# Mixture of eight expert MLPs on one core: x in four loads of 1, 1, 2 and 4 experts, stores in pairs, late results stored on the GpSimd queue

## The chip, the cores and the metric

The kernel runs on one core of a Trainium2 chip. The metric is device time in microseconds (us), the median of several executions. Five executions of the kernel before took 183.25 to 184.44 us, with a median of 184.28.

## What is computed

Eight experts each apply a two-layer MLP to their own 256 rows. Everything is float32 in memory.

```python
n_experts, capacity, hidden, expert_hidden = 8, 256, 512, 2048
# x: (8, 256, 512)   w1: (8, 512, 2048)   w2: (8, 2048, 512)
h = np.matmul(x, w1)
h = np.maximum(h, 0)
out = np.matmul(h, w2)          # (8, 256, 512) float32
```

## The kernel before

**Data and types.** The matmuls run in bf16. A weight matrix is 4.2 MB of float32 in memory; a DMA issued from GpSimd (`nc.gpsimd.dma_start`, POOL in the profile) converts it to bf16 on the way, so that 2048 KB arrive on the chip. `load_w1` (L60) and `load_w2` (L66) each issue such a load, into pools of three buffers (`WB = 3`). `load_w2` cuts the matrix of expert 6 into 3 pieces and that of expert 7 into 7, the last three of one k-tile (128 KB on the chip) each; all others are one load.

**x.** The eight experts' x is treated as two groups of four experts (`G = 2`). Group 0, 2 MB of float32, is loaded by SP (L132) into `x_f`, 16 KB in a row for each partition, and ACT converts it to bf16 in four casts (L142). Group 1 is loaded and converted by a GpSimd DMA (L137). `transpose_x` (L74) turns a group around on TensorE: 32 transposes of 128x128 for a group, and two copies (L87 on ACT, L89 on DVE) for each of four k-tiles, into `xt`.

**Compute.** `first_layer(e)` (L91) makes 64 matmuls of 128x256 (L97) for an expert; DVE and ACT take turns at the ReLU (L105, L107). `second_layer(e)` (L111) makes 32 matmuls of 128x512 (L117) over 16 k-tiles; DVE and ACT each copy one half of the result (L125, L126) into `o_sb[e]`, from a pool of five buffers.

**Order.** The schedule is written out by hand (`manual_schedule`): each engine executes its instructions in program order, and each queue takes its DMAs in the order of issue. All weights, x group 1 and the results of experts 0 to 4 (`store`, L128) share the one GpSimd queue, called q0 in the profile; SP's queue is q1 and ACT's q10. The order on GpSimd is: w1(0), the identity matrix (two short instructions), w2(0), w1(1), x group 1, w2(1), w1(2), w2(2); then w1(3), w2(3), store 0, w1(4), w2(4), store 1, w1(5), w1(6), w1(7), w2(5), store 2, w2(6) in pieces, store 3, store 4, w2(7) in pieces. A load into a used buffer waits until the matmuls that read it are done, and a DMA on GpSimd also waits for the landing of the eighth DMA before it on this queue, or of a later one, since eight semaphores are used in turn.

TensorE runs the layers expert by expert up to first layer 4, second layer 4, then first layers 5, 6, 7, then second layers 5, 6, 7. The four transposed k-tiles of x group 1 stand between the matmuls of first layer 2.

**The end.** The results of experts 5 and 6 are stored by SP (L179), with a dependency by hand on the third last weight piece, `pieces[-3]`; the result of expert 7 goes out in halves, from SP (L188) and ACT (L189).

Of the kernel before, what the change touches and what calls it, by code (L numbers as in the profile page):

```python
# [1 line left out]

# [5 lines left out]


@with_exitstack  # L10
def kernel(
    ctx: ExitStack,
    tc: tile.TileContext,
    x: bass.AP,
    w1: bass.AP,
    w2: bass.AP,
    out: bass.AP,
):
    nc = tc.nc
    P = 128  # L20
    bf = mybir.dt.bfloat16
    f32 = mybir.dt.float32
    relu = mybir.ActivationFunctionType.Relu

    E, C, H = x.shape
    F = w1.shape[2]
    MT = C // P
    KT1 = H // P
    KT2 = F // P
    G = 2  # L30
    EG = E // G
    J = EG * C // P
    J2 = J // MT
    WB = 3


    x_r = x.rearrange("(g e) c k -> g (e c) k", g=G).rearrange(
        "g (p j) k -> g p j k", p=P
    )
    w1_r = w1.rearrange("e (p kt) n -> e p kt n", p=P)  # L40
    w2_r = w2.rearrange("e (p kt) n -> e p kt n", p=P)
    out_r = out.rearrange("e (p mt) n -> e p mt n", p=P)

    const = ctx.enter_context(tc.tile_pool(name="const", bufs=1))
    wpool = ctx.enter_context(tc.tile_pool(name="weights", bufs=WB))
    hpool = ctx.enter_context(tc.tile_pool(name="hidden", bufs=3))
    opool = ctx.enter_context(tc.tile_pool(name="outs", bufs=5))
    ps_h = ctx.enter_context(tc.tile_pool(name="ps_h", bufs=4, space=bass.MemoryType.PSUM))
    ps_o = ctx.enter_context(tc.tile_pool(name="ps_o", bufs=4, space=bass.MemoryType.PSUM))


    ctx.enter_context(tc.manual_schedule())

    w1_sb, w2_sb, ht, o_sb = {}, {}, {}, {}
    x_f = const.tile([P, J, H], f32, name="x_f")
    x_b = [const.tile([P, J, H], bf, name=f"x_b{g}") for g in range(G)]
    xt = [const.tile([P, KT1, EG, C], bf, name=f"xt{g}") for g in range(G)]
    identity = const.tile([P, P], bf, name="identity")

    def load_w1(e):  # L60
        w1_sb[e] = wpool.tile([P, KT1, F], bf, tag="w1", name="w1_sb")
        nc.gpsimd.dma_start(w1_sb[e][:], w1_r[e])  # L62

    pieces = []

    def load_w2(e):  # L66
        w2_sb[e] = wpool.tile([P, KT2, H], bf, tag="w2", name="w2_sb")
        cuts = {E - 2: (0, 6, 11, 16), E - 1: (0, 4, 8, 11, 13, 14, 15, 16)}.get(e, (0, KT2))
        for lo, hi in zip(cuts, cuts[1:]):
            pieces.append(  # L70
                nc.gpsimd.dma_start(w2_sb[e][:, lo:hi, :], w2_r[e, :, lo:hi, :])  # L71
            )

    def transpose_x(g, kts):  # L74


        for kt in kts:
            pt = ps_o.tile([P, J, P], bf, tag="ps_o", name="pt_tr")
            for j in range(J):
                nc.tensor.transpose(pt[:, j, :], x_b[g][:, j, kt::KT1], identity[:])  # L80
            src = pt[:].rearrange("p (j m) (e l) -> p m e l j", m=MT, e=EG)
            for mt in range(MT):
                dst = xt[g][:, kt, :, mt * P:(mt + 1) * P].rearrange(
                    "p e (l j) -> p e l j", j=J2
                )
                if mt % 2:
                    nc.scalar.copy(dst, src[:, mt])  # L87
                else:
                    nc.vector.tensor_copy(dst, src[:, mt])  # L89

    def first_layer(e, between=()):  # L91
        ht[e] = hpool.tile([P, KT2, C], bf, tag="ht", name="ht_sb")
        for g in range(KT2 // 2):
            ph = ps_h.tile([P, 2, C], f32, tag="ps_h", name="pt_h")
            for i in range(2):
                for kt in range(KT1):
                    nc.tensor.matmul(  # L97
                        ph[:, i, :],
                        w1_sb[e][:, kt, 2 * g + i::KT2],
                        xt[e // EG][:, kt, e % EG, :],  # L100
                        start=(kt == 0),
                        stop=(kt == KT1 - 1),
                    )
            if g % 2:
                nc.vector.tensor_relu(ht[e][:, 2 * g:2 * g + 2, :], ph[:])  # L105
            else:
                nc.scalar.activation(ht[e][:, 2 * g:2 * g + 2, :], ph[:], relu)  # L107
            if g % 2 and between:
                between.pop(0)()

    def second_layer(e):  # L111
        po = [
            ps_o.tile([P, H], f32, tag="ps_o", name=f"pt_o{mt}") for mt in range(MT)
        ]
        for kt in range(KT2):
            for mt in range(MT):
                nc.tensor.matmul(  # L117
                    po[mt][:],
                    ht[e][:, kt, mt * P:(mt + 1) * P],
                    w2_sb[e][:, kt, :],  # L120
                    start=(kt == 0),
                    stop=(kt == KT2 - 1),
                )
        o_sb[e] = opool.tile([P, MT, H], f32, tag="o", name="out_sb")
        nc.vector.tensor_copy(o_sb[e][:, 0, :], po[0][:])  # L125
        nc.scalar.copy(o_sb[e][:, 1, :], po[1][:])  # L126

    def store(e):  # L128
        nc.gpsimd.dma_start(out_r[e], o_sb[e][:])  # L129


    nc.sync.dma_start(x_f[:], x_r[0])  # L132
    load_w1(0)
    make_identity(nc, identity)
    load_w2(0)
    load_w1(1)
    nc.gpsimd.dma_start(x_b[1][:], x_r[1])  # L137
    load_w2(1)
    load_w1(2)
    load_w2(2)  # L140
    for j in range(0, J, 2):
        nc.scalar.copy(x_b[0][:, j:j + 2, :], x_f[:, j:j + 2, :])  # L142
    transpose_x(0, range(KT1))

    first_layer(0)
    load_w1(3)
    second_layer(0)
    load_w2(3)
    store(0)
    first_layer(1)  # L150
    load_w1(4)
    second_layer(1)
    load_w2(4)
    store(1)
    first_layer(2, [lambda kt=kt: transpose_x(1, [kt]) for kt in range(KT1)])
    load_w1(5)
    second_layer(2)
    first_layer(3)
    load_w1(6)
    second_layer(3)  # L160
    first_layer(4)
    load_w1(7)
    load_w2(5)
    store(2)
    load_w2(6)
    store(3)
    second_layer(4)
    store(4)
    load_w2(7)


    for e in (5, 6, 7):
        first_layer(e)
    for e in (5, 6, 7):
        second_layer(e)


    for e in (5, 6):
        d = nc.sync.dma_start(out_r[e], o_sb[e][:])  # L179
        tc.add_manual_dep(  # L180
            d.ins,
            pieces[-3].ins.name,
            mybir.DependencyInfo(
                mybir.DependencyClass.Sync, mybir.DependencyReason.SCHED_ONLY
            ),
            reason="after the weights",
        )
    nc.sync.dma_start(out_r[7, :, 0, :], o_sb[7][:, 0, :])  # L188
    nc.scalar.dma_start(out_r[7, :, 1, :], o_sb[7][:, 1, :])  # L189


# [1 line left out]
_INS = ['x', 'w1', 'w2']  # L193
_OUTS = [((8, 256, 512), 'float32')]


# [23 lines left out]
```

## Time and profile before

| | |
|---|---|
| median of five executions | 184.28 us (183.25 to 184.44) |
| the profiled execution | 184.44 us |
| its span, first to last instruction | 182.2 us |
| mean granted TensorE clock | 0.911 of full speed |
| moved by DMA, as counted on the chip's side | 41.00 MB, mean 225 GB/s |
| read from memory; written to it | 71.30 MB; 4.19 MB |
| share of the 16 DMA engines: q0 (GpSimd); q1 (SP); q10 (ACT) | 93.9%; 5.0%; 0.4% |
| x_f, SP's load of x: issue to landing | 12.7 us |
| w1(0), the first weights: issue at 1.24 us, to landing | 17.0 us |
| first matmul of first layer 0 | 20.13 us |
| last weight piece: issue at 165.87 us, to landing | 11.0 us |
| last matmuls of second layer 7 | end at 178.12 us |
| ACT's half of result 7: issue at 178.76 us, to landing | 2.6 us |

Some execution time lies outside the span: 184.44 against 182.2 here. In the profile's rows an instruction's line number is that of the kernel file. The 40 slices of part 2 cover 4.55 us each; PEclk is the clock that TensorE was granted, and the DMA row the mean busy share of the 16 DMA engines, both in tenths. GB/s counts a converted weight with the bytes that arrive, half of those that are read. The DMA share can exceed 1 a little, because an engine's packets overlap. A DMA issue (DMA_DIRECT2D) on POOL takes about 0.53 us of that engine; the transfer itself follows on the queue.

### The profile page before, as it was taken

The numbers are of one execution on the slowest core, as the hardware profiler recorded it, in microseconds if no ns is written. First come the engines' busy times: TensorE is split into PE (matmuls) and PEld (weight loads), VectorE is DVE, ScalarE is ACT, GpSimd is POOL, SyncE is SP. The second block draws the span as 40 slices with busy tenths as digits, with TensorE's granted clock in tenths as the row PEclk, the third lists the DMA queues.
The fourth block names the chain that finished last, engine by engine and source line by source line (L and its number), as shares of the span: only waits on it lengthen the run. The fifth ranks groups of instructions, "written<-read, shape, count | busy, mean of one in ns | idle before, by whom it ended". The sixth has DMA issues, their size and how long they took to land.

```text
span 182.2 us, 1878 instructions
## 1 busy us (share of the span) xinstructions
PE 131.3 (72%) x825; PEld 91.0 (50%) x832; DVE 32.8 (18%) x48; ACT 33.4 (18%) x53; POOL 16.7 (9%) x36
## 2 busy tenths in 40 slices
PE   0004899759039998949968299937999597996890
PEld 0002795359013597418833279416998495442340
DVE  0000541113100155011301014010343033011001
ACT  2008531113000135011301022011223031011001
POOL 7200001110100101000000000601010101112000
PEclk9999999999956999996999759995799799999698
DMA  6999999999999999999899999999999999999986
GB/s 198 309 259 212 230 223 205 207 212 239 205 209 227 223 216 198 227 227 223 190 274 212 201 230 277 212 205 227 223 219 194 227 230 244 213 279 256 205 202 232
DMA packets 5047, 41.00 MB, mean 225 GB/s; under 512 B 560, under 2 KB 944, under 8 KB 2992
## 3 DMA queue, kind: packets, MB, share of 16 engines
q0 software_dynamic: 4320, 37.23, 93.9%
q1 hardware_dynamic: 576, 3.41, 5.0%
q10 hardware_dynamic: 144, 0.26, 0.4%
q8 instruction: 6, 0.10, 0.2%
q14 instruction: 1, 0.01, 0.0%
HBM read 71.30 MB, written 4.19 MB: 414 GB/s over the span
## 4 chain that ended last, share of the span: by engine, by line
DMA 57%; PE 33%; another core or an unknown queue 5%; POOL 1%; issue 1%; ACT 0%; POOLq 0%
DMA w_sb<-in_w_dram 57%; PE pt_o L117 18%; PE pt_h L97 14%; PE pt_tr L80 1%; POOL w_sb L62 1%; ACT out_sb L126 0%; POOL w_sb L71 0%; POOL x_b L137 0%; POOL identity masks.py:199 0%; POOL identity masks.py:197 0%; POOLq masks.py:199 0%; POOLq L71 0%; POOLq L204 0%
## 5 line engine op out<-in xcount | busy, mean ns | idle before, releaser
L97 PE MATMUL pt_h<-xt,w_sb 128*128 128x256 bf16 x512 | 66.5, 295 | 17.0 <-DMA w_sb<-in_w_dram 16.1
L97 PEld LDWEIGHTS <-w_sb 128*128 128x128 bf16 x512 | 60.3, 148 | 23.8 <-DMA w_sb<-in_w_dram 18.8
L117 PE MATMUL pt_o<-w_sb,ht_sb 128*128 128x512 bf16 x249 | 59.9, 397 | 13.6 <-DMA w_sb<-in_w_dram 13.1
L117 PEld LDWEIGHTS <-ht_sb 128*128 128x128 bf16 x256 | 25.9, 102 | 45.8 <-issue 16.8
L105 DVE TENSOR_SCALAR ht_sb<-pt_h 128x512 bf16<-128x512 f32 x32 | 22.1, 692 | 61.3 <-PE pt_h L97 61.3
L107 ACT ACTIVATE ht_sb<-pt_h 128x512 bf16<-128x512 f32 x32 | 19.1, 598 | 54.4 <-PE pt_h L97 54.4
L80 PE MATMUL pt_tr<-identity,x_b 128*128 128x128 bf16 x64 | 6.6, 264 | 16.2 <-ACT x_b L142 16.2
L126 ACT COPY out_sb<-pt_o 128x512 f32<-128x512 f32 x8 | 4.7, 586 | 71.9 <-PE pt_o L117 71.9
L125 DVE COPY out_sb<-pt_o 128x512 f32<-128x512 f32 x8 | 5.5, 692 | 66.2 <-PE pt_o L117 66.2
L80 PEld LDWEIGHTS <-x_b 128*128 128x128 bf16 x64 | 5.4, 127 | 16.9 <-ACT x_b L142 16.9
L71 POOL DMA_DIRECT2D w_sb<-in_w_dram x16 | 8.6, 541 | 50.4 <-DMA w_sb<-in_w_dram 26.1
L62 POOL DMA_DIRECT2D w_sb<-in_w_dram x8 | 4.4, 552 | 81.4 <-PE pt_h L97 80.6
L89 DVE COPY xt<-pt_tr 128x512 bf16<-128x512 bf16 x8 | 5.5, 686 | 18.3 <-PE pt_tr L80 18.3
L142 ACT CAST x_b<-x_f 128x1024 bf16<-128x1024 f32 x4 | 3.9, 1042 | 11.4 <-DMA x_f<-in_x_dram 11.4
L87 ACT COPY xt<-pt_tr 128x512 bf16<-128x512 bf16 x8 | 4.7, 585 | 7.0 <-DVE xt L89 7.0
L129 POOL DMA_DIRECT2D out_dram<-out_sb x5 | 2.7, 539 | 17.6 <-DMA w_sb<-in_w_dram 17.0
L142 ACT ACT_TABLE_LOAD x1 | 1.3, 1283 | 0.7 <-PEq L204 0.7
L137 POOL DMA_DIRECT2D x_b<-in_x_dram x1 | 0.5, 547 | 0.0
masks.py:199 POOL TENSOR_SCALAR_AFFINE_SELECT identity<-identity 128x128 bf16<-128x128 bf16 x1 | 0.3, 287 | 0.1
masks.py:197 POOL MEMSET identity<- 128x128 bf16 x1 | 0.2, 223 | 0.0
L204 POOL MEMSET const-float32-0.0<- 128x1 f32 x1 | 0.1, 98 | 0.2 <-issue 0.2
L204 POOL MEMSET const-bfloat16-1.0<- 128x1 bf16 x1 | 0.1, 101 | 0.0
(2 smaller groups left out, 0.2 us busy)
## 6 DMA issues: line engine op xcount, KB each, us to landing
w_sb<-in_w_dram POOLq DMA_DIRECT2D x14, 2048.0 KB, 49.6
out_dram<-out_sb POOLq DMA_DIRECT2D x5, 512.0 KB, 41.0
x_f<-in_x_dram SPq DMA_DIRECT2D x1, 2048.0 KB, 12.7
w_sb<-in_w_dram POOLq DMA_DIRECT2D x2, 640.0 KB, 46.6
x_b<-in_x_dram POOLq DMA_DIRECT2D x1, 1024.0 KB, 39.8
w_sb<-in_w_dram POOLq DMA_DIRECT2D x2, 512.0 KB, 21.9
out_dram<-out_sb SPq DMA_DIRECT2D x2, 512.0 KB, 3.1
w_sb<-in_w_dram POOLq DMA_DIRECT2D x1, 768.0 KB, 42.8
```

The lines of the kernel that those rows point to most:

```text
L62: nc.gpsimd.dma_start(w1_sb[e][:], w1_r[e])
L71: nc.gpsimd.dma_start(w2_sb[e][:, lo:hi, :], w2_r[e, :, lo:hi, :])
L80: nc.tensor.transpose(pt[:, j, :], x_b[g][:, j, kt::KT1], identity[:])
L87: nc.scalar.copy(dst, src[:, mt])
L89: nc.vector.tensor_copy(dst, src[:, mt])
L97: nc.tensor.matmul(ph[:, i, :], w1_sb[e][:, kt, 2 * g + i::KT2], xt[e // EG][:, kt, e % EG, :], start=(kt == 0), stop=(kt == KT1 - 1),)
L105: nc.vector.tensor_relu(ht[e][:, 2 * g:2 * g + 2, :], ph[:])
L107: nc.scalar.activation(ht[e][:, 2 * g:2 * g + 2, :], ph[:], relu)
L117: nc.tensor.matmul(po[mt][:], ht[e][:, kt, mt * P:(mt + 1) * P], w2_sb[e][:, kt, :], start=(kt == 0), stop=(kt == KT2 - 1),)
L125: nc.vector.tensor_copy(o_sb[e][:, 0, :], po[0][:])
L126: nc.scalar.copy(o_sb[e][:, 1, :], po[1][:])
L142: nc.scalar.copy(x_b[0][:, j:j + 2, :], x_f[:, j:j + 2, :])
```

## The change

Four things change.

- **x** comes in four groups, of 1, 1, 2 and 4 experts. Group 0, 512 KB of float32, is loaded by SP, 4 KB in a row for each partition, and converted by one cast on ACT. Groups 1, 2 and 3 are GpSimd loads that convert, each into a buffer of its own, placed behind w1(0), behind w1(1) and behind w2(1). Each group is transposed by itself: group 1 after first layer 0, group 2 after first layer 1, group 3 between the matmuls of first layer 2. An expert has the same bytes of x and as many transposes as before.
- **Stores** of experts 0 and 1, 2 and 3, 4 and 5 are joined into one DMA each, from an output buffer for two experts (a pool of four such buffers instead of five single ones).
- **Results of 4, 5 and 6** are stored on the GpSimd queue after all pieces of w2(7); expert 4's store stood ahead of w2(7), and 5 and 6 were on SP. The dependency by hand goes. Expert 7 is stored as before.
- **Pieces**: w2(6) comes in 2 pieces instead of 3, w2(7) in 6 (5, 4, 3, 2, 1, 1 k-tiles) instead of 7.

The order of the GpSimd queue becomes w1(0), x1, w2(0), w1(1), x2, w2(1), x3, w1(2), w2(2), w1(3), w2(3), w1(4), w2(4), store 0+1, w1(5), w1(6), w1(7), w2(5), store 2+3, w2(6), w2(7), store 4+5, store 6. With the same eight semaphores, w2(2) is now the ninth DMA and waits for the landing of w1(0). The matmuls, their sizes and their order are those of before, except for the place of the transposes.

```diff
-    G = 2
-    EG = E // G
-    J = EG * C // P
-    J2 = J // MT
+    GROUPS = ((0, 1), (1, 1), (2, 2), (4, 4))
+    STORES = ((0, 1), (2, 3), (4, 5), (6,), (7,))
...
-    out_r = out.rearrange("e (p mt) n -> e p mt n", p=P)
+    out_r = out.rearrange("e (p mt) n -> p e mt n", p=P)
...
-    opool = ctx.enter_context(tc.tile_pool(name="outs", bufs=5))
+    opool = ctx.enter_context(tc.tile_pool(name="outs", bufs=4))
...
-    x_f = const.tile([P, J, H], f32, name="x_f")
+    x_f = const.tile([P, MT, H], f32, name="x_f")
...
+    def x_rows(g):
+        e0, n = GROUPS[g]
+        return x[e0:e0 + n].rearrange("e c k -> (e c) k").rearrange(
+            "(p j) k -> p j k", p=P
+        )
+
+    def load_x(g):
+        nc.gpsimd.dma_start(x_b[g][:], x_rows(g))
...
-        cuts = {E - 2: (0, 6, 11, 16), E - 1: (0, 4, 8, 11, 13, 14, 15, 16)}.get(e, (0, KT2))
+        cuts = {E - 2: (0, 8, 16), E - 1: (0, 5, 9, 12, 14, 15, 16)}.get(e, (0, KT2))
...
-        o_sb[e] = opool.tile([P, MT, H], f32, tag="o", name="out_sb")
-        nc.vector.tensor_copy(o_sb[e][:, 0, :], po[0][:])
-        nc.scalar.copy(o_sb[e][:, 1, :], po[1][:])
+        es = next(es for es in STORES if e in es)
+        if e == es[0]:
+            o_sb[es] = opool.tile([P, 2, MT, H], f32, tag="o", name="out_sb")
+        o = o_sb[es][:, e - es[0]]
+        nc.vector.tensor_copy(o[:, 0, :], po[0][:])
+        nc.scalar.copy(o[:, 1, :], po[1][:])
...
-    nc.sync.dma_start(x_f[:], x_r[0])
+    nc.sync.dma_start(x_f[:], x_rows(0))
     load_w1(0)
     make_identity(nc, identity)
+    load_x(1)
     load_w2(0)
     load_w1(1)
-    nc.gpsimd.dma_start(x_b[1][:], x_r[1])
+    load_x(2)
     load_w2(1)
+    load_x(3)
     load_w1(2)
     load_w2(2)
-    for j in range(0, J, 2):
-        nc.scalar.copy(x_b[0][:, j:j + 2, :], x_f[:, j:j + 2, :])
-    transpose_x(0, range(KT1))
+    nc.scalar.copy(x_b[0][:], x_f[:])
+    transpose_x(0)
...
-    store(2)
+    store(2, 3)
     load_w2(6)
-    store(3)
     second_layer(4)
-    store(4)
     load_w2(7)
...
-    for e in (5, 6, 7):
-        second_layer(e)
-    for e in (5, 6):
-        d = nc.sync.dma_start(out_r[e], o_sb[e][:])
-        tc.add_manual_dep(
...
+    second_layer(5)
+    store(4, 5)
+    second_layer(6)
+    store(6)
+    second_layer(7)
+    o = o_sb[(7,)]
+    nc.sync.dma_start(out_r[:, 7, 0, :], o[:, 0, 0, :])
+    nc.scalar.dma_start(out_r[:, 7, 1, :], o[:, 0, 1, :])
```

## The prediction

> **What bounds the kernel now.** I read the page first: the shares of part 1, the 40 slices of part 2, the chain of part 4.
>
> ```profile
> PE 131.3 (72%) x825; PEld 91.0 (50%) x832; DVE 32.8 (18%) x48; ACT 33.4 (18%) x53; POOL 16.7 (9%) x36
> ...
> PE   0004899759039998949968299937999597996890
> ...
> DMA  6999999999999999999899999999999999999986
> ...
> DMA 57%; PE 33%; another core or an unknown queue 5%; POOL 1%; issue 1%; ACT 0%; POOLq 0%
> ```
>
> TensorE is busy 72% of the span, but the DMA row is 8 or 9 in every slice except the first and the last. The chain names weight loads for 57%. So the 16 DMA engines are the bound from the first load to the last store, and work on other engines is worth nothing unless it changes when those engines have something to do. The change moves the same bytes (x 4.19 MB read, results 4.19 MB written, weights 67.1 MB read as f32), so only idle DMA time and order can change the end. I therefore asked for the DMA share by stretches at both ends (columns: length, the engines' busy time, PEclk, DMA share, GB/s):
>
> ```profile
> 0.00:1.70 1.70, 0.00 (x0) 0.00 (x0) 0.00 (x0) 0.97 (x1) 0.67 (x5) 1.00 0.00 0
> 1.70:3.20 1.50, 0.00 (x0) 0.00 (x0) 0.00 (x0) 0.32 (x1) 1.43 (x5) 1.00 1.07 240
> 3.20:5.40 2.20, 0.00 (x0) 0.00 (x0) 0.00 (x0) 0.00 (x0) 2.20 (x5) 1.00 0.98 410
> ...
> 174.40:176.40 2.00, 2.00 (x11) 0.88 (x9) 0.00 (x0) 0.00 (x0) 0.00 (x0) 1.00 0.45 73
> 176.40:179.20 2.80, 1.71 (x8) 0.59 (x6) 0.69 (x1) 0.59 (x1) 0.00 (x0) 1.00 0.94 375
> 179.20:181.10 1.90, 0.00 (x0) 0.00 (x0) 0.00 (x0) 0.00 (x0) 0.00 (x0) 0.87 0.74 276
> ```
>
> DMA is busy from 1.7 us. The only soft places are 174.4 to 176.4 (0.45) and the last two microseconds (0.74). Then I asked which queue fills the first stretch (DMA view of 1.7 to 5.4, then of 5.5 to 6 us):
>
> ```profile
> q1 hardware_dynamic: 77, 1.26, 101.5%
> ```
>
> ```profile
> q0 software_dynamic: 12, 0.20, 185.7%
> q1 hardware_dynamic: 2, 0.03, 15.8%
> ```
>
> Up to 5.4 us every packet belongs to the SP load of x; the GpSimd queue (q0), which carries all weights, shows its first packets only then, although its first issue stands at 1.24 us:
>
> ```profile
> 0.74 0.37 SPq L132 DMA_DIRECT2D x_f<-in_x_dram  x1
> 1.24 0.66 POOL L62 DMA_DIRECT2D w_sb<-in_w_dram  x1 [0.79 <-POOLq L204]
> ```
>
> The 2 MB load of x is thus what the engines live on before the weights come.
>
> **The change part by part.**
>
> *The first load of x, 512 KB instead of 2 MB.* At the rates above it moves 1.5 us x 240 GB/s = 0.36 MB by 3.2 us and the other 0.16 MB in 0.4 us: done at 3.6 us. If the first weights still come at 5.4, the DMA engines idle 1.8 us, and the 0.74 MB of x that moved in that time in the old kernel must be moved later, on a stream that is full. A packet of 16 KB takes 16384 x 16 / 410 GB/s = 0.64 us, and q0 had to wait on average half of one for its turn, 0.3 us, which a free engine doesn't need. I take **+1.5 us**. Both ends: nothing (q0 was ready by 3.6 and only sat behind x packets already under way) and +2.4 us (q0 gets its first turn when the opening burst of GpSimd issues is over: in the trace of before it ends at 5.05 + 0.57 = 5.62 us, close to the first packets; the changed kernel issues 8 DMAs in that burst instead of 7, at 0.53 us each).
>
> The Trainium skill, "DMA: Bandwidth & Descriptors", section Specifications, gives about 1 us of first-byte latency for a GpSimd DMA. By that q0 would be ready near 2.9 us and the gap would be nothing, so that the sum would end below the old time; the trace has 4.2 us from issue to first packet, but with the other queue in the way, so it does not refute the page.
>
> *The other loads of x on GpSimd.* They carry 0.52, 1.05 and 2.1 MB of f32 where one carried 2.1 MB; with the SP load it is the same total. Two more DMAs in this place, one fewer piece each of expert 6's and expert 7's weights, and four GpSimd stores instead of five: the number of DMAs on the queue falls from 30 to 29. I take 0, bounds -0.4 and +0.4 us. The two extra POOL issues (0.53 each) are hidden by the queue's backlog: the fourth w1 load is issued at 28.85 and its matmuls start at 82.07, 53 us later. If that cover were gone, each would cost its 0.53.
>
> *TensorE and copies.* First layer 0 can start some 5 us earlier (x no longer shares the queue with w1); 8, 8, 16 and 32 transposes replace 32 and 32, at 264 ns each; ACT casts once (1.04 us) instead of four times. Nothing of it reaches the end: 9.7 us of weights for each layer of an expert stand against about 7 us of matmuls, and the matmuls of L97 and L117 wait 16.1 and 13.1 us for weights in all. A slot that comes free earlier only lengthens the backlog. The order of instructions puts one new wait on POOL: the load of expert 2's w2 now waits for the landing of the first w1, about 15 us. Behind it stands only the fourth w1 load, which waits for first layer 0 anyway. I take 0; it would cost only if the queue ran dry, with 50 us on it.
>
> *The store of expert 4, behind the last weights.* In the old kernel it stood ahead of them. What a store is worth on the queue: matmuls of w2(3) start at 92.44 and those of w1(4), with store 0 between, at 103.42: 10.98 us, against 9.69 from 53.00 to 62.69 without one: **1.3 us**. So the last weights land 1.3 us earlier than the old 176.87 (issue 165.87 + 11.0 to landing): 175.6.
>
> *What follows the last weights.* Then come experts 4, 5 (2.6 us) and 6 (1.3 us) on the same queue, and expert 7 from SP and ACT (31.7% and 31.8% of 2.2 us, 0.7 each). That is 5.3 us: the last store lands at 180.9 if nothing waits. The old one landed at 178.76 + 2.57 = 181.33 (ACT's 256 KB, 2.6 us to landing). So **-0.4 us**. The gain is small because the old stores of 5 and 6, held on SP until 175.60 by the wait on a weight piece, already ran right behind the last weights (0.94 of 176.4 to 179.2). Expert 7 must be ready in time: its last two matmuls, 0.43 us, ACT's copy 0.59 and 1.4 us from issue to first packet end near 178.3, before the queue is done with expert 6 at 179.2 (175.6 less the 0.35 us that a landing takes, plus 3.9). With PEclk at one half in second layer 7, as from 170.4 to 173.8 now, TensorE needs 8.8 us instead of 6.9 from its first piece (9.69 x 11/16 = 6.7 us before the last one) and ends 1.9 us later than the weights: then the end is 181.0, still within this term. Bounds -1.0 and +0.3. SP loses a wait of 174.4 us that nobody waited for. The two new waits stand on POOL: the store of 4 and 5 for the copies of second layer 5 (done at 160.7 now), the store of 6 for those of layer 6 (167.6 now, a microsecond or two later with expert 6's weights in two pieces). Behind them POOL has nothing, and both are early against 175.6; a later store would leave the queue empty for the difference.
>
> *Sum:* 184.44 (the profiled run, span 182.2) + 1.5 + 0 + 0 - 1.3 + 0.84 (the 5.3 us after the weights against 181.33 - 176.87 = 4.46 now) = 185.5. That run lies 0.16 above the median of five, 184.28; on the median it is **185.3**, which I give.
>
> **Rivals.**
>
> *The weights come sooner (slower forecast fails).* GpSimd's first load is ready by 3.6 us and merely queued behind x. For it: SP's own first packet comes about 1 us after its issue, and at the end ACT's q10 shows few packets before q1 is nearly through, though issued 0.11 us after it. Against it: q0 and q1 do take turns packet by packet from 5.5 on. The gap is then 0 and the time 184.3 - 0.4 = 183.9. It decides as soon as the gap is under 0.4 us.
>
> *The queue opens after the burst of issues.* Gap 2.4: 184.3 + 2.4 - 0.4 = 186.3. For it: first packets at 5.4 to 6, the last issue ending at 5.62. Against it: one q0 packet before 5.5.
>
> *The late engines are not late.* From 174.4 to 176.4 the share is 0.45: most of the 16 engines are through with the weights while some still work, and the old SP stores start at 176.4 on all together. The new stores follow at once on each engine. If the laggards are not the same ones at the end, half of that stretch, 1.1 us, comes back: 184.3 - 0.4 - 1.1 = 182.8 without the gap, 184.3 with one of 1.5.
>
> **How the numbers follow.** A measurement of this kernel tells about 0.5% (0.9 us) from no change. Forecast, gap 1.2 to 1.8: 0.50, 184.9 to 185.8. Early weights: 0.25, 183.6 to 184.4. After the burst: 0.15, 185.9 to 186.6. Laggards: 0.10, 182.6 to 184.3. Leaving out the ends gives 183.6 to 186.5. Slower by over 0.5% means above 185.2: a bit over half of the forecast and all of the burst case, 0.44; faster means under 183.4: most of the laggards and a little of the early case, 0.11; the rest, 0.45, lies between. The likeliest case stands on that boundary, so the two are nearly even.
>
> **What would show it.** Right: the DMA share drops near 0 between 3.6 and 5.4 us; q0's first packets at 5 to 5.5; first layer 0 starts at 15 to 15.5 instead of 20.1; last weights land at 176.9 to 177.3; DMA share 0.9 or more up to the last store. Wrong: q0 packets at 3 to 4 us; a hole in the DMA row in the middle; a final store that starts after expert 6 is already through; or an end set by the copy of expert 7 and not by DMA.

## The result, and the profile after

The changed kernel takes 184.02 us (median of 53 executions, 182.69 to 185.04), the kernel before 183.68 us (95 executions, 182.85 to 184.54). The ratio is 1.0014, 95% interval [1.0005, 1.0024]: slower by some 0.26 us (the two medians lie 0.34 apart). The forecast was 185.3, that is +1.0 us on a median of five executions, 184.28, which itself lay 0.6 us above the median of 95. The direction was right, the size was three to four times too large. The times of the changed kernel also spread over 2.35 us, those of before over 1.7.

The profiled execution took 183.18 us (span 181.4), one of the shorter ones, while the profile of before, at 184.44, was one of the longest. A comparison of these two traces alone would have said that the change wins 1.3 us. From the page of the changed kernel:

```profile
PE 127.9 (71%) x825; PEld 90.2 (50%) x832; DVE 32.9 (18%) x56; ACT 31.2 (17%) x58; POOL 16.8 (9%) x35
...
PE   0206979499491299979687696926999494997980
...
DMA  6989999999999999999999998999999999999994
...
DMA 59%; PE 28%; another core or an unknown queue 8%; POOL 1%; issue 1%; ACT 0%; POOLq 0%
```

The DMA engines remain the bound, and there is no hole in their row (the last slice, 4, is the end). The same stretches of the span as before (length, engines' busy time, PEclk, DMA share, GB/s):

```profile
1.70:3.20 1.50, 0.00 (x0) 0.00 (x0) 0.00 (x0) 0.32 (x1) 1.43 (x5) 1.00 0.96 300
3.20:5.40 2.20, 0.17 (x2) 0.18 (x3) 0.00 (x0) 1.04 (x1) 2.20 (x5) 1.00 1.30 257
...
174.40:176.40 2.00, 1.72 (x8) 0.58 (x6) 0.46 (x1) 0.25 (x1) 0.00 (x0) 1.00 1.04 409
176.40:179.20 2.80, 0.00 (x0) 0.00 (x0) 0.23 (x1) 0.34 (x1) 0.00 (x0) 1.00 0.86 340
179.20:181.10 1.90, 0.00 (x0) 0.00 (x0) 0.00 (x0) 0.00 (x0) 0.00 (x0) 0.64 0.12 44
```

The stretch from 3.2 to 5.4, where the forecast saw idle engines, is full (1.30; the share counts a packet whole in the stretch where it starts, so it can pass 1). The soft place from 174.4 to 176.4 has gone from 0.45 to 1.04. The queues between 1.7 and 5.4 us show who fills the start:

```profile
q0 software_dynamic: 30, 0.49, 72.2%
q1 hardware_dynamic: 144, 0.52, 43.9%
```

The GpSimd queue, with no packet before 5.4 us in the old kernel, has 30 here; the first stands at 3.28 us, while SP's last packets of x run (the last ends at 3.73).

### The profile page after: what moved, and what is told of

Its sections match the earlier page's. It is cut to its first block, busy times and chain, and to the rows that moved or that the text cites. A ratio compares the mean times of both kernels' runs of the same rounds, so it can differ in the third digit from the quotient of the medians.

```text
span 181.4 us, 1880 instructions
## 1 busy us (share of the span) xinstructions
PE 127.9 (71%) x825; PEld 90.2 (50%) x832; DVE 32.9 (18%) x56; ACT 31.2 (17%) x58; POOL 16.8 (9%) x35
## 3 DMA queue, kind: packets, MB, share of 16 engines
HBM read 71.30 MB, written 4.19 MB: 416 GB/s over the span
## 4 chain that ended last, share of the span: by engine, by line
DMA 59%; PE 28%; another core or an unknown queue 8%; POOL 1%; issue 1%; ACT 0%; POOLq 0%
DMA w_sb<-in_w_dram 59%; PE pt_h L105 14%; PE pt_o L125 13%; PE pt_tr L86 1%; POOL x_b L66 1%; ACT out_sb L137 0%; POOL w_sb L70 0%; POOL w_sb L76 0%; POOL identity masks.py:199 0%; POOL identity masks.py:197 0%; POOLq L208 0%
## 5 line engine op out<-in xcount | busy, mean ns | idle before, releaser
L105 PE MATMUL pt_h<-xt,w_sb 128*128 128x256 bf16 x512 | 67.6, 299 | 30.7 <-DMA w_sb<-in_w_dram 30.7
L125 PE MATMUL pt_o<-w_sb,ht_sb 128*128 128x512 bf16 x249 | 56.4, 379 | 12.3 <-DMA w_sb<-in_w_dram 10.5
L125 PEld LDWEIGHTS <-ht_sb 128*128 128x128 bf16 x256 | 24.8, 98 | 42.2 <-issue 9.9
L76 POOL DMA_DIRECT2D w_sb<-in_w_dram x14 | 7.5, 539 | 67.2 <-DMA w_sb<-in_w_dram 41.3
L70 POOL DMA_DIRECT2D w_sb<-in_w_dram x8 | 4.5, 559 | 73.0 <-PE pt_h L105 52.5
L86 PE MATMUL pt_tr<-identity,x_b 128*128 128x128 bf16 x64 | 5.6, 242 | 5.2 <-ACT x_b L154 5.2
L93 ACT COPY xt<-pt_tr 128x128 bf16<-128x128 bf16 (+2 forms) x16 | 5.4, 376 | 9.6 <-DVE xt L95 9.6
L95 DVE COPY xt<-pt_tr 128x128 bf16<-128x128 bf16 (+2 forms) x16 | 5.6, 385 | 5.8 <-PE pt_tr L86 5.8
L66 POOL DMA_DIRECT2D x_b<-in_x_dram x3 | 1.7, 563 | 0.0
L154 ACT CAST x_b<-x_f 128x1024 bf16<-128x1024 f32 x1 | 1.0, 1044 | 2.1 <-DMA x_f<-in_x_dram 2.1
```

The lines of the kernel that those rows point to most:

```text
L66: nc.gpsimd.dma_start(x_b[g][:], x_rows(g))
L105: nc.tensor.matmul(ph[:, i, :], w1_sb[e][:, kt, 2 * q + i::KT2], xe[:, kt, :], start=(kt == 0), stop=(kt == KT1 - 1),)
L125: nc.tensor.matmul(po[mt][:], ht[e][:, kt, mt * P:(mt + 1) * P], w2_sb[e][:, kt, :], start=(kt == 0), stop=(kt == KT2 - 1),)
```

## The experiments

Kernels of one group share a chip and the executions of before on it (medians 183.59, 183.87, 183.68 and 183.86 us in the four groups). The diffs are against the changed kernel; what follows from them (the size of `x_f`, its casts, the places of the transposes) is left out.

**First group: the parts one by one.** Two kernels carry one part of the change each, one undoes the pieces, one takes SP out of the start.

`x_only`: the changed x, everything else as before.

```diff
-    STORES = ((0, 1), (2, 3), (4, 5), (6,), (7,))
+    STORES = tuple((e,) for e in range(E))
...
-        cuts = {E - 2: (0, 8, 16), E - 1: (0, 5, 9, 12, 14, 15, 16)}.get(e, (0, KT2))
+        cuts = {E - 2: (0, 6, 11, 16), E - 1: (0, 4, 8, 11, 13, 14, 15, 16)}.get(e, (0, KT2))
...
-    store(4, 5)
...
-    store(6)
...
+    for e in (5, 6):
+        d = nc.sync.dma_start(out_r[:, e], o_sb[(e,)][:, 0])
...
```

> Only the x part of the change: four groups of x, with stores, pieces and end as before. The prediction on record: +1.5 us for a gap of 1.8 us in the DMA row before 5.4 us. Theory 'start': no gap (the weights' first packets come at about 3.3 us), but some engines are late from the first load on because the weights' first packets now meet the slow first microseconds that x met before: +0.4 to +0.7 us, ratio 1.002 to 1.004. Rival 'end': the start is neutral, ratio 0.999 to 1.001.

185.02 us (6 executions, 184.15 to 186.03), ratio 1.0085 [1.0055, 1.0116]. No gap in the trace: the first weight packet comes at 3.39 us.

```profile
3.20:4.60 1.40, 0.00 (x0) 0.00 (x0) 0.00 (x0) 0.39 (x1) 1.40 (x4) 1.00 1.21 281
4.60:6.40 1.80, 1.04 (x8) 0.78 (x8) 0.65 (x4) 1.04 (x3) 1.55 (x3) 1.00 1.33 273
```

So the gap is refuted, and yet the x part costs twice what theory 'start' gave it, and as much as the forecast had put on the gap.

`stores_only`: the changed stores, x and pieces as before.

```diff
-    GROUPS = ((0, 1), (1, 1), (2, 2), (4, 4))
+    GROUPS = ((0, 4), (4, 4))
...
-    cuts = {E - 2: (0, 8, 16), E - 1: (0, 5, 9, 12, 14, 15, 16)}
+    cuts = {E - 2: (0, 6, 11, 16), E - 1: (0, 4, 8, 11, 13, 14, 15, 16)}
```

> Only the stores: pairs, and results 4 to 6 on the GpSimd queue behind the last weights, with x and pieces as before. Theory 'start': the worked-out -0.4 us of the end shows, ratio 0.997 to 0.999. Rival 'end': the stores on the GpSimd queue run on each engine at its own pace, the last engine is late with them, and the end loses 0.2 to 0.5 us: ratio 1.001 to 1.003, with a wide spread of times.

183.30 us, ratio 0.9988 [0.9974, 1.0001], spread 1.0 us. As theory 'start' has it, though the interval just reaches 1; the rival 'end' fails in sign and in spread.

`no_sp_x`: x of expert 0 on the GpSimd queue as well.

```diff
-    nc.sync.dma_start(x_f[:], x_rows(0))
     load_w1(0)
+    load_x(0)
...
-    nc.scalar.copy(x_b[0][:], x_f[:])
```

> The changed kernel with x group 0 on the GpSimd queue too, behind the first weights, converted by the DMA; SP loads nothing, ACT's cast goes. It shows when the GpSimd queue is ready with nothing in its way. The prediction on record needs a first packet near 5 us; the other case a first packet by 3.3 us or earlier. If it comes later than 1.75 us, when SP's first packet came, the DMA row shows that gap and the time is longer than the changed kernel's by the gap: about +1.3 us for a first packet at 3.0 to 3.3, less the 0.5 MB of x that is not moved by SP (same bytes, so no credit).

183.90 us, ratio 1.0018 [1.0005, 1.0032]. The first weight load's issue, from the timeline of this kernel, and then its stretches:

```profile
1.26 0.67 POOL L69 DMA_DIRECT2D w_sb<-in_w_dram  x1 [0.81 <-POOLq L206]
```

```profile
1.70:2.60 0.90, 0.00 (x0) 0.00 (x0) 0.00 (x0) 0.32 (x1) 0.90 (x3) 1.00 0.00 0
2.60:4.50 1.90, 0.00 (x0) 0.00 (x0) 0.00 (x0) 0.00 (x0) 1.82 (x5) 1.00 0.99 147
```

Nothing moves until 2.6 us, then the weights do: 1.37 us from issue to first packet. The GpSimd queue is ready at 2.6 us, not at 5.4. The second row holds another thing: engines busy at 0.99 but only 147 GB/s, where the same stream later brings 209 (4.60 to 6.40); all 16 first packets took 1.37 to 2.09 us instead of 1.23. The 0.9 us of gap were expected to cost 1.3 us against the changed kernel and cost nothing: a miss, and a sign that the changed kernel loses as much in another way.

`old_cuts`: the changed kernel with the old pieces.

```diff
-    cuts = {E - 2: (0, 8, 16), E - 1: (0, 5, 9, 12, 14, 15, 16)}
+    cuts = {E - 2: (0, 6, 11, 16), E - 1: (0, 4, 8, 11, 13, 14, 15, 16)}
```

> The changed kernel with the old pieces of experts 6 and 7 (3 and 7 instead of 2 and 6). Both theories: within 0.2 us of the changed kernel; two more DMAs cost 8 packets of some 20 ns on each engine each.

184.37 us (183.30 to 185.87), ratio 1.0039 [1.0010, 1.0068]. Against the changed kernel's 1.0014 [1.0005, 1.0024] that is inconclusive. With `stores_only`, from which it differs in x alone, it gives the x part a second time: +1.07 us.

**Second group: how long SP's load is.** The changed kernel once more, and three that differ in x alone.

`after_again`: no edit.

> The changed kernel once more, for a second trace and more times beside the same runs of before. Its median lay 0.26 us above before (ratio 1.0014). Theory 'start' and its rivals alike: 1.000 to 1.004. If the trace is of one of the longer executions (184.5 and up), theory 'start' expects that the last engine's landing of the first weights is over 1.4 us behind the first engine's, against 0.8 us in before; the rival (a late engine is hit by an instruction fetch, a packet of 0.93 us, on its way) expects the same 0.8 to 1.4 at the start and one or two further steps of 0.9 us later.

184.57 us, ratio 1.0019 [0.9994, 1.0043]; its trace is of an execution of 184.58 us. The last of the 16 engines landed the first weights 2.37 us after the first one, 1.43 in the trace of 183.18 us. That is as theory 'start' expected. The rival's step is there too: between 103 and 113 us the landings spread by another 1.1 us, and an instruction fetch stands at 107.1.

`sp_1mb`: SP loads two experts.

```diff
-    GROUPS = ((0, 1), (1, 1), (2, 2), (4, 4))
+    GROUPS = ((0, 2), (2, 2), (4, 4))
```

> The changed kernel with SP's load of x at 1 MB (groups of 2, 2 and 4 experts). Stores and pieces as changed. Theory 'start' (what costs is that the weights meet the slow first microseconds): between 512 KB (184.0 to 184.4) and 2 MB (183.3), 183.4 to 183.9. Rival 'GpSimd loads' (the x loads between the weights cost, not the start): near 184, since two of three remain.

183.36 us, ratio 0.9967 [0.9955, 0.9980], spread 0.8 us: theory 'start', just under its range. First weight packets at 4.84 to 5.13 us, all of 1.23 to 1.28 us; the engines' landings of the first weights lie within 0.26 us. They did not stay so close: at the last weights they are 2.8 us apart in this trace (183.81 us, the longest of the twelve).

`gp_split`: SP loads four experts as before, the GpSimd loads are three.

```diff
-    GROUPS = ((0, 1), (1, 1), (2, 2), (4, 4))
+    GROUPS = ((0, 4), (4, 1), (5, 1), (6, 2))
```

> SP loads 2 MB of x (experts 0 to 3) as before; experts 4 to 7 come in three GpSimd loads of 1, 1 and 2 experts at the places where the changed kernel has its three. Stores and pieces as changed. Theory 'start': as with the stores alone, 183.0 to 183.5, ratio 0.997 to 0.999. Rival 'GpSimd loads': as the changed kernel, 184.0 to 184.4.

182.73 us (6 executions), ratio 0.9933 [0.9917, 0.9950]: the rival fails, since the GpSimd loads between the weights cost nothing. Theory 'start' missed as well, by 0.3 us: this version is faster than both kernels.

`sp_three`: SP brings the same 2 MB in three loads, x of expert 0 first.

```diff
-    nc.sync.dma_start(x_f[:], x_rows(0))
+    for g in range(3):
+        nc.sync.dma_start(x_f[g][:], x_rows(g))
...
-    load_x(1)
...
-    load_x(2)
```

> The changed kernel, but x groups 0, 1 and 2 (512 KB, 512 KB, 1 MB) all come from SP, in three loads, and ACT casts them; group 3 stays on GpSimd. SP's queue is then busy for 2 MB again, while x of expert 0 is still early. Theory 'start': 183.0 to 183.5. Rival 'row size' (rows of 4 KB in the first load make the spread): 183.9 to 184.4.

183.55 us, ratio 0.9984 [0.9970, 0.9998]: between the two. Weight packets come at 4.6 us, eight of them slow (1.33 to 1.83 us).

**Third group: time or length, rows, pieces.**

`w1_late`: the first weights come later, behind the same short load of x.

```diff
+    scratch = const.tile([P, 1024], f32, name="scratch")
+    for _ in range(2):
+        nc.gpsimd.memset(scratch[:], 0.0)
     load_w1(0)
```

> The changed kernel with two memsets of a scratch tile on GpSimd ahead of the first weight load, so that the first weight packet comes at 4.6 to 5.2 us instead of 3.3, with SP's 512 KB of x through at 3.7. A gap of about 1.2 us appears in the DMA row. Theory 'early packets' (weight packets are slow only if they begin before about 4.6 us): no first packet over 1.3 us, times within 0.8 us of each other, median 184.3 to 184.7 (the 1 MB kernel's 183.36 plus 1.2 for the half MB not moved). Rival 'short load' (weights behind a short x load are slow whenever they come): first packets of 1.4 to 2.4 us again, times spread over 2 us, median 185 or more.

183.95 us, ratio 1.0018 [1.0001, 1.0036], spread 1.1 us. The memsets were shorter than planned, so that the first packets came at 4.01 to 4.80 us, partly outside the window to be tested. All 16 were slow, 1.56 to 2.16 us, those after 4.6 too, but slow alike: the landings lie within 0.65 us. Its stretches:

```profile
3.70:4.00 0.30, 0.00 (x0) 0.00 (x0) 0.00 (x0) 0.00 (x0) 0.30 (x2) 1.00 0.00 0
4.00:5.80 1.80, 0.66 (x7) 0.66 (x8) 0.22 (x2) 1.04 (x1) 1.80 (x4) 1.00 1.04 146
```

A true gap, and then 146 GB/s, as in the kernel without SP's load. Neither theory holds as it was put: the 'early packets' did not become fast, and the 'short load' did not bring back the wide spread.

`sp_1mb_4k`: 1 MB from SP, in rows of 4 KB.

```diff
-    nc.sync.dma_start(x_f[:], x_rows(0))
+    nc.sync.dma_start(x_f[:], x[0:2].rearrange("e (p j) k -> p e j k", p=P))
...
-    load_x(1)
```

> The changed kernel, but SP's one load carries experts 0 and 1 (1 MB) in rows of 4 KB; groups 2 and 3 stay on GpSimd. If the row size matters, first weight packets come sooner than with 1 MB in 8 KB rows (4.84 us) and some are slow: 183.6 to 184.4. If only the bytes matter: as there, 183.1 to 183.6.

183.18 us, ratio 0.9961 [0.9944, 0.9977], no slow weight packet: with 1 MB the rows of 4 KB do no harm, so it is the bytes that matter.

`stores_pieces`: stores and pieces changed, x as before.

```diff
-    GROUPS = ((0, 1), (1, 1), (2, 2), (4, 4))
+    GROUPS = ((0, 4), (4, 4))
```

> x as before (2 MB on SP, one GpSimd load of 2 MB), stores and pieces as changed. The stores alone gave 183.3. If the pieces matter: 182.7 to 183.0, as with the split GpSimd loads; if it is the split of the GpSimd loads that brought 182.73, 183.2 to 183.5.

183.36 us, ratio 0.9980 [0.9962, 0.9998]: the pieces bring nothing that can be told from zero. Its spans are 181.1 us in the median, those of `gp_split` 180.9; most of the 0.6 us between the two lies outside the span.

`gp_split_again`: no edit to `gp_split`.

> The version with 2 MB of x on SP, three GpSimd loads for experts 4 to 7, stores and pieces as changed, once more: six runs gave 182.73. All theories: 182.5 to 183.2, ratio 0.992 to 0.997.

182.74 us, ratio 0.9944 [0.9924, 0.9964].

**Fourth group: where the lateness starts.** Three single executions of the changed kernel, and one with shorter first packets.

> The changed kernel, one execution with its trace. Theory 'late engines': between executions, the time rises about as much as the wait from the first engine's landing of the first weights to the last engine's (1.43 us at 183.18, 2.37 at 184.58), so within 0.4 us of 183.2 + 1.4 x (wait - 1.43) / 0.94. Rival 'later hits' (what differs comes after the first weights): no relation, with two executions of equal wait over 0.7 us apart.

> As the run before it: one more execution of the changed kernel, the same relation expected by theory 'late engines', none by 'later hits'.

> As the two runs before it: one more execution of the changed kernel, the same relation expected by theory 'late engines', none by 'later hits'.

They took 184.57, 183.94 and 184.84 us at waits of 1.98, 2.61 and 2.83 us. The relation to the wait gave 184.0, 185.0 and 185.3: missed three times, by more than the 0.4 us allowed. But the wait starts at the first engine, and in `after_t3` that one is late too (14.56 us instead of 13.6). What orders the five traces better is the landing of the first weights itself, which is that of the last engine. From the DMA view of its issue, in the trace of 183.18 us and in the one of 184.84:

```profile
w_sb<-in_w_dram POOLq DMA_DIRECT2D x1, 2048.0 KB, 13.8
```

```profile
w_sb<-in_w_dram POOLq DMA_DIRECT2D x1, 2048.0 KB, 15.2
```

The last column is the time from issue to landing. The others have 15.0 (183.94), 15.3 (184.57) and 15.3 (184.58). From this landing to the end of the last weight packet it is 160.1, 159.7, 160.0, 159.9 and 160.4 us, from the shortest execution to the longest, and from there to the last packet of all 5.03 us in each. So of the 1.66 us between the shortest and the longest of these executions, some 1.4 are there when the first weights land. This relation was read from these traces; the one stated ahead of them failed. It rests mainly on the one short execution: the other four lie 0.9 us apart in time and 0.3 us in landing.

`w1_quarters`: the first weights in four loads.

```diff
+        step = 1 if e == 0 else KT1
+        for lo in range(0, KT1, step):
+            nc.gpsimd.dma_start(w1_sb[e][:, lo:lo + step, :], w1_r[e, :, lo:lo + step, :])
```

> The changed kernel with the first weights in four loads of one k-tile, so that their packets are a quarter as long; three more DMAs cost three times 8 packets of some 20 ns on each engine, 0.2 us in all with their completion. If a slow first packet costs a fixed time, the lateness stays and the time is as the changed kernel's, 184.0 to 184.8. If it is proportional to the packet, or shorter packets even out between engines, the spread falls under 1 us and the median to 183.2 to 183.7.

184.44 us (183.54 to 185.60), ratio 1.0027 [0.9999, 1.0055]; its trace, of 185.15 us, has landings of the first quarter 3.1 us apart. Shorter packets don't take the lateness away.

## Why the prediction was wrong

**The gap (+1.5 us), the step that failed.** "If the first weights still come at 5.4, the DMA engines idle 1.8 us." They come at 3.2 to 3.5 us in the five traces. The row of before (4.2 us from issue to first packet) was read as the queue's own latency, but SP's packets stood in its way: with nothing there it is 1.37 us (`no_sp_x`; `w1_late`, where SP is through before it, gives 1.37 again). The rival 'the weights come sooner' was right about the queue, but its sum, a gain of 0.4 us, was not: 184.02 lies in its range only because the level of before was taken 0.6 us too high. The figure of the Trainium skill, "DMA: Bandwidth & Descriptors", Specifications (about 1 us for GpSimd), had pointed there too; the runs give 1.37.

**What stands in its place.** The x part still costs: +1.4 us (`x_only` against before), +1.07 (`old_cuts` against `stores_only`), +0.6 (the changed kernel against `stores_pieces`, by the ratios; +1.1 in the span). In the old kernel the first weights land at 1.24 + 17.0 = 18.2 us, with 1.57 MB more of x by then; at 0.433 MB per us (4.19 MB in 9.69 us) that is worth 3.6 us, so 14.6 would be even. The changed kernel's five traces have 15.0, 16.2, 16.4, 16.5 and 16.5: late by 0.4 to 1.9 us. In each trace two to six of the 16 engines land 1 to 2.8 us behind the first, and some of the first weight packets took 1.9 to 2.8 us instead of 1.23. The trace names no engine, so that the slow packets are those of the late engines is inferred. In the kernels where SP loads 1 or 2 MB in one DMA, no weight packet before 8 us took over 1.3. In the five traces the late engines do not catch up: the landings are 1.4 to 2.8 us apart at the first weights, 2.2 to 3.7 at the last.

The traces of other kernels, put beside this count afterwards, each with its own bytes of x, mostly agree: `gp_split` lands even and has a span of 180.9 us; `old_cuts`, 0.3 early, has 181.5; `w1_late` and `no_sp_x`, 0.7 to 0.8 late, 182.2 and 182.6; the changed kernel, 1.6 to 1.9 late in four traces, 182.1 to 183.0. `sp_1mb` does not: it lands 0.6 early and has 181.9, since its engines drift apart later.

So a cost of about the size of the +1.5 us was paid, not in an empty stretch but, as far as these traces show, by late engines, and in a varying amount, which would be the wide spread. That the forecast had the right direction is luck: its gap does not exist. Why a weight stream that begins behind half a megabyte of x is slow unevenly (and slow but even when it begins on idle engines) is not settled. The packet's length does not decide it (`w1_quarters`), nor do rows of 4 KB (`sp_1mb_4k`), nor GpSimd's burst of issues, which in `sp_1mb` runs on until 6.21 us over fast packets. Nor is it the time since the issue alone: packets begun 1.4 to 2.5 us after it were all slow in `no_sp_x` and `w1_late`, those from 3.6 us on were fast in the 1 MB kernels, but `after_again` has packets of 1.6 to 1.9 us begun 4.7 to 5.1 us after it.

**The end (-0.4 us).** The mechanism held, and the size too: in the span the new stores win 0.25 us (`stores_only`, 181.25 against 181.5 of before in its group) and, with the new pieces, 0.5 (`stores_pieces`, 181.1 against 181.6). In the trace of before and in `x_only`, which keeps the old stores, the last packet of all ends 4.46 us after the last weight packet; in all traces with the new stores, whatever the start, 5.03 (5.3 was forecast). With the store of expert 4 behind the weights (8 packets of 0.16 us on each engine, 1.28) that would be worth 1.28 - (5.03 - 4.46) = 0.71 us, somewhat more than the spans show. Expert 7's halves, from the timeline of the changed kernel, were issued while the queue still worked on expert 6, as forecast:

```profile
176.66 0.35 SPq L192 DMA_DIRECT2D out_dram<-out_sb  x1
176.77 0.37 ACTq L193 DMA_DIRECT2D out_dram<-out_sb  x1
```

The old end, for comparison, in the windows of `x_only`:

```profile
174.40:176.40 2.00, 2.00 (x11) 0.91 (x10) 0.00 (x0) 0.00 (x0) 0.00 (x0) 1.00 0.64 103
176.40:179.20 2.80, 1.76 (x9) 0.59 (x6) 0.69 (x1) 0.59 (x1) 0.00 (x0) 1.00 0.94 376
```

The dip before 176.4 is that of before (0.45 there). The engines that idle there must be the early ones, which would be why filling the dip wins less than its area (1.1 us). The rival 'the late engines are not late' fails: it needed a gain of 1.5 us at the end, where `stores_only` and `stores_pieces` show 0.25 and 0.5.

**The terms at nothing** (other x loads, TensorE, POOL's new wait) held: `gp_split` has the three GpSimd loads and is the fastest; first layer 0 starts at 15.07 instead of 20.13 us in the trace of 183.18, and nothing comes of it. The pieces stay within their bounds.

**The sum.** In the span the changed kernel has a median of 182.2 us and before 181.5 to 181.8: about +0.6, against the +1.04 forecast. `stores_pieces`, which differs from the changed kernel in x alone, splits it: x costs 182.2 - 181.1 = 1.1 us in the span, where the gap was to cost 1.5, and stores and pieces win 0.5, where 0.46 was forecast. Outside the span the changed kernel has 1.78 us in the median, before 2.1 (1.8 to 2.3), `stores_pieces` 2.28. That -0.3 against before was no term of the sum, and its cause is in no trace. Together: 1.1 - 0.5 - 0.3 = +0.3. So the forecast was too large because the start costs 0.4 less and 0.3 lie outside the span. The absolute time missed by another 0.6, since five executions of before were taken for its level.

## What to carry to other kernels

A long time from issue to first packet is a latency only if the DMA engines were free; where another queue filled them, it says only when the turn came, so take the free case as one end before building a gap on it. On a kernel bound by DMA the last engine sets the end: in the five traces of the changed kernel, what late engines lost in the first microseconds was still missing at the end, and filling idle time of the early ones brought half a microsecond at most. But engines that start together can drift apart later too, by 2.5 us in `sp_1mb`. Compare traces only beside the times of many executions: here two single traces had the wrong sign.

## What was not expected of the hardware

- The first packets of a weight stream took 1.4 to 2.2 us instead of 1.23 where they began on idle engines (`no_sp_x`, `w1_late`), and up to 2.8 us, unevenly, behind 512 KB of x; behind 1 MB or 2 MB in one load none did.
- With 2 MB of x on SP, the GpSimd queue (ready at 2.6 us in `no_sp_x`) got its first packet at 5.3 to 5.7 us; with 1 MB at 4.8 to 5.0.
- An instruction fetch is one packet of 16 KB on queue q8 that takes 0.9 us of one engine, six times in each trace. Where one seems to have struck a late engine, the spread of landings grew by about 1 us (`after_t5`: from 2.83 to 3.91).
